# Router, shift vectors and attention combination of a transformer block on one Trainium2 core: three re-orderings and one change of engine

## The chip, the cores and the metric

The kernel runs on one core of a Trainium2 chip. The metric is device microseconds of one execution. The engines are TensorE (PE, with its weight loads shown as PEld), VectorE (DVE), ScalarE (ACT), GpSimd (POOL) and SyncE (SP), which issues most DMAs. All of them run at the same time, each in the order of its own queue, and wait for one another through semaphores.

## The reference

One block of a diffusion transformer, batch 1, 1024 tokens of width 2048 and 256 context tokens. A conditioning vector c is turned by a large matrix `w_ada` (2048 x 12288) into six modulation vectors (shift, scale and gate for two halves); the context has its own c_ctx. Then:

```
mod_x = (silu(c) @ w_ada + b_ada)            # six vectors of 2048; [0] shift, [1] scale
mod_c = (silu(c_ctx) @ w_ada + b_ada)
hx = rmsnorm(x, norm1_g) * (1 + mod_x[1]) + mod_x[0]      # hc the same with mod_c
q, k, v, p, gb, gc, xin = split(hx @ w_in)   # k, v for the context too; q, k turned by rope
# differential attention, 8 heads, two maps each, over 1280 keys
a = softmax(q k / 8);  w = a[map 0] - lam * a[map 1];  att = w @ v
mix = concat(rmsnorm(att), pool_mix(p), gb * conv(gc * xin)) @ w_out
x = x + mod_x[2] * mix
h2 = rmsnorm(x, norm2_g) * (1 + mod_x[4]) + mod_x[3]
aff = softmax(h2 @ w_router)                 # 16 experts
g, idx = top_k(aff.T, 128)                   # each expert takes its 128 best tokens
y = scatter_add(idx, g * (silu(xg @ w_gate) * (xg @ w_up)) @ w_down)
out = rmsnorm(x + mod_x[5] * y, final_g)
```

## The kernel before, in words

Products are made in a split form: an fp32 operand is cut into a high part (ACT copies it to the matmul's type) and a low part (DVE or POOL subtracts), and three products high-high, low-high and high-low stand for one. The weights of the in-projection come in units of 512 KB (`w_unit`, L414: a DMA `w_raw` by SP, an ACT copy L419, a subtraction L420 on an engine that the caller names), two buffers deep.

**In-projection.** Its work is cut into chunks of 128 output columns (`ChunkA`); a chunk has 16 steps, one for each 128 rows of width, and each step has six products `g_x` on 768 token columns (nine with the context columns). The first two chunks run while the inputs and the scale vectors arrive. The scale vectors are made by `ada_block` (L281 to L291): PE multiplies loads of w_ada column by column as they come (`ada_ps`, column-tiled: four products of 32 columns each side by side in one bank), ACT copies the bank to `ada_s`, and four small products `ada_pc` turn it into columns. Next come six plain chunks without the shift (P2, P3, and GB0 to GB3), then K, V, Q, GC and X chunks, in which four extra columns of the token operand hold the shift vectors (`shift_columns`), so that the bias of a chunk comes out of the same products. The shift vectors must therefore be there before the first K chunk. Here they are made by `ada_shift(j)`, j = 0, 1, through `weighted_rows`: 32 loads of 128 x 1024, of which DVE accumulates column 0 (L304) and, for the context, ACT scales (L307) and POOL adds (L308); then 4 x 8 PE transposes (`ada_t`, L314) and DVE sums. `next_rows` starts the next such list. After them come `bias_late`, and the later modulation vectors beside the K to X chunks.

**Attention.** 64 steps (head, block of 256 queries, half of it). A step i does a list of operations taken from `T["even"]`, `T["odd"]`, or for the last 18 steps `T["late"]` and `T["lato"]`: `S` is `score(i + 2)` (PE products `sc` of both maps, DVE maximum `nm` L947, ACT exponential `e` L952), `C` is `combine(i + 2)` (DVE: reciprocal `cf` L959, two small operations, the multiply-add of the two maps L964), `T0` to `T2` transpose step i's combined map (`turn`: `trw`, `wth`, `wtl`), `V` multiplies with v, and a number is a share of filling: pieces of the out-projection and of the pool and conv features that PE does in between. Each `nm` is held behind the last multiply-add by an order edge (`nosync`).

**Router.** Four blocks of 256 tokens: `ln2(b)` normalises (L1279, L1280), transposes and multiplies with the router's weights (`rl`), and `affinity(b)` copies the logits (`lg`), turns them by products with `sel16` (the second `rl`), adds the mean's part (`rsm` L1257), exponentiates, scales (L1265) and turns back (L1266). All of these products share one PSUM buffer, tag `rl`. In front of the first, `rls` is a product of ones with the weights' column sums `sws` (L1236). PE fills the gaps with the out-projection (`fill(n)`: n pieces, a token piece being three or more products `gm`). Top-k runs on DVE in two parts: over the first three blocks (`top(0)`, L1341 to L1350, 768 wide) and over the last and the merge (`top(1)`). Then `chosen` is the list of tokens, which an indirect DMA gathers (L1469).

**Experts.** 16 experts, three matrices each, come as 512 KB or 1 MB loads and are split like the others (ACT L1409, DVE or POOL L1413, `es_t`); the first pieces are prepared before the gather ends. `split` takes four of them on POOL and the rest on DVE.

**Order.** Each engine's order is made by a planner that simulates a time line: of the instructions that are ready, the one that comes first in the program goes first. `nosync` adds an order without a semaphore.

Of the kernel before, what the change touches and what calls it, by code (L numbers as in the profile page):

```python
# [20 lines left out]
P = 128  # L21
# [46 lines left out]
    adm=2,  # L68
# [7 lines left out]
    sh1=0,  # L76
    sh2=0,
# [10 lines left out]
    pin=1,  # L88
    nsy=1,
# [75 lines left out]
def block_kernel(tc, I, out, dbg=None):  # L165
# [127 lines left out]
    def weighted_rows(wap, c0, cols):  # L293

        accs = [p.tile([P, 1024], F32, name="ada_a", tag="ada_a", bufs=1) for _, _, p, _ in cols]
        for k in range(KT):
            wt = wt_pools[ada_n[0] % len(wt_pools)].tile([P, 1024], F32, name="ada_w", tag="ada_w")
            ada_n[0] += 1
            sp.dma_start(wt, wap[k * P:(k + 1) * P, c0:c0 + 1024])
            for (col, eng, _, _), a in zip(cols, accs):  # L300
                if k == 0:
                    act.activation(a, wt, AF.Copy, scale=col(k))
                elif eng is dve:
                    dve.scalar_tensor_tensor(a, wt, col(k), a, op0=ALU.mult, op1=ALU.add)  # L304
                else:
                    t = adx.tile([P, 1024], F32, name="ada_m", tag="ada_m", bufs=T["adm"])
                    act.activation(t, wt, AF.Copy, scale=col(k))  # L307
                    eng.tensor_tensor(a, a, t, op=ALU.add)  # L308
# [13 lines left out]
    def ada_shift(j):  # L322
        ks = slice(8 * j, 8 * j + 8)
        yield from weighted_rows(w_ada, j * 1024, [(lambda k: st[:, k, 0:1], dve, ev, mods[:, 0, ks]),
                                                   (lambda k: st[:, k, 1:2], gp, adx, modc[:, 0, ks])])
        for m in (mods, modc):
            dve.tensor_tensor(m[:, 0, ks], m[:, 0, ks], b_col[:, ks], op=ALU.add)
# [140 lines left out]
    adx = mk("adx", bufs=1, side="left")  # L468
# [93 lines left out]
    rows_left = [ada_shift(0), ada_shift(1), bias_late()] + [ada_late(m, j) for m in (2, 3, 4, 5) for j in range(2)]  # L562
# [12 lines left out]
    next_rows()  # L575
    for n, (g, off, dst) in enumerate([(2, OFF_P, pS), (3, OFF_P, pS)] + [(g, OFF_GB, gbS) for g in range(4)]):
        finish_plain(run_chunk(off + g * P, False, False), dst[g])
        if n == T["sh1"]:
            next_rows()
        if n == T["sh2"]:  # L580
            next_rows(False)
            shift_columns()
            next_rows()
    for h in range(HEADS):
        finish_k(run_chunk(OFF_K + h * P, True), h)
        if h % 2:
            next_rows()
        if h == 0:
            mk.close("adx")
            wt_pools[2:] = [mk("adw", bufs=T["adw"], side="left")] * T["adw"]  # L590
# [87 lines left out]
    pos = {"job": 0, "unit": 0, "tick": 0, "gen": None, "half": 0, "pool": None}  # L678
# [15 lines left out]
    def features(parts, finish, hook):  # L694
# [4 lines left out]
        for u in range(2):  # L699
            s = next_unit()  # L700
            for kk in range(8):
                hi, lo = parts[2 * u + kk // 4]
                for wl, hh in ((0, hi), (0, lo), (1, hi)):
                    one = mm(o, s[:, wl, kk, :], hh[:, kk % 4, :], start=(n == 0), stop=(n == 3 * KT - 1))
                    nosync(tc, one, pos["pin"])
                    n += 1
# [5 lines left out]
    def tokens(b, c, hook):  # L712
# [3 lines left out]
        for j in MIX_ORDER:  # L716
            s = next_unit()
            for kk in range(4):
                n += 1
                hi, lo = mix_parts[b][j]  # L720
                for qt in range(2):
# [4 lines left out]
                    mm(o[:, qt], lo[:, kk, t], s[:, 0, kk, :], start=False, stop=(n == KT))  # L726
# [422 lines left out]
    if True:  # L1149
# [14 lines left out]
        for i in range(LEAD):  # L1164
            score(i)
            fill(T["f3"])
            combine(i)
        want = [0.0]
        waiting = None
        for i in range(NS):  # L1170
# [16 lines left out]
            for op in T[("late" if late else "even") if qt == 0 else ("lato" if late else "odd")]:  # L1187
# [14 lines left out]
                elif op == "C" and nxt:  # L1202
                    combine(nxt)
# [36 lines left out]
    dve.tensor_copy(S2W, t[:, 0:NE])  # L1240
# [6 lines left out]
    def affinity(b, rl):  # L1247
# [16 lines left out]
        for qt in range(2):  # L1264
            dve.tensor_scalar(sm[:, qt], sm[:, qt], sc_[:, 4 + qt:5 + qt], None, op0=ALU.mult)  # L1265
            pe.transpose(r3[0:NE, qt * P:(qt + 1) * P], sm[:, qt], ident)  # L1266
        dve.tensor_copy(affT[:, b * QB:(b + 1) * QB], r3[0:NE, 0:QB])

    def ln2(b):
# [21 lines left out]
        affinity(b, rl)  # L1291
# [112 lines left out]
    def split(i, kk, early=None):  # L1404
        if i < len(units) and (i, kk) not in splits:
# [8 lines left out]
            if early and not on_gp:  # L1414
                nosync(tc, lo, early)
# [32 lines left out]
    for i in range(2):  # L1448
        for kk in range(2):
            split(i, kk, chosen)  # L1450
# [182 lines left out]
```

## Time and profile before

| | us |
|---|---|
| median of three runs | 3376.15 (3362.58 to 3376.82) |
| profiled run | 3386.7 |
| its span, first to last instruction | 3384.9 |
| PE busy | 3084.9 (91%) |
| DVE busy | 2350.6 (69%) |
| ACT busy | 1808.5 (53%) |
| POOL busy | 963.3 (28%) |
| mean granted clock of PE | 0.954 of full speed |

Read by stage (us of the span): input and scale vectors to 93, the first two chunks to 111, six plain chunks to 250, the K to X chunks to about 915, attention to 1896, router to 2155, experts to the end. In the columns of the window view PEclk is the granted clock of PE as a share of full speed, and DMA share is the mean busy share of the 16 DMA engines.

### The profile page before, as it was taken

The page shows a single profiled execution, that of the slowest core. Times are in us where ns is not written, and L with a number is a line of the kernel's source. Part 1 is how long each engine was busy: PE and PEld are TensorE (multiplying, and loading weights), DVE is VectorE, ACT ScalarE, POOL GpSimd, SP SyncE. Part 2 cuts the span into 40 slices and gives each one's busy share as a digit, 9 for nine tenths or more (in the row PEclk, how much of TensorE's full clock was granted, in tenths as well). Part 3 has the DMA queues.
Part 4 walks back from the last instruction along what each step waited for, and adds up shares of the span by engine and source line. Part 5 has one row for each costly group of instructions (what it writes and reads, how often), then busy time and mean ns, then how long its engine had stood idle before and what let it go on. Part 6 is the DMA issues. An engine that isn't in the chain of part 4 may idle for free. (4 is left out here: it accounts for less than half of the span.)

```text
span 3384.9 us, 48355 instructions
## 1 busy us (share of the span) xinstructions
PE 3084.9 (91%) x18527; PEld 2650.1 (78%) x18527; DVE 2350.6 (69%) x2778; ACT 1808.5 (53%) x2585; POOL 963.3 (28%) x608
## 2 busy tenths in 40 slices
PE   7789999999978889888989989599999999999996
PEld 5678989888867778777989879478877777777774
DVE  5666765662157666666555479789888888878877
ACT  5433422362245555554445344577766677667665
POOL 1551100010245544544666576320000000000021
PEclk9899999999989899988999999799999999999998
DMA  9668777732465554646777876899999999999998
GB/s 322 189 184 274 266 261 253 255 124 91 118 188 171 156 160 141 183 130 219 226 258 249 284 261 199 336 342 376 382 374 367 369 358 370 358 370 369 352 328 317
DMA packets 489562, 891.22 MB, mean 263 GB/s; under 512 B 24913, under 2 KB 339874, under 8 KB 478450
## 3 DMA queue, kind: packets, MB, share of 16 engines
q1 hardware_dynamic: 465488, 791.42, 66.9%
q0 software_dynamic: 23744, 96.68, 9.3%
q8 instruction: 145, 2.38, 0.3%
q14 instruction: 87, 0.71, 0.1%
q10 hardware_dynamic: 98, 0.03, 0.0%
HBM read 797.80 MB, written 90.23 MB: 262 GB/s over the span
## 5 line engine op out<-in xcount | busy, mean ns | idle before, releaser
L1413 DVE TENSOR_TENSOR es_t<-er_t,es_t 128x1024 fp32r<-128x1024 f32 x764 | 892.3, 1221 | 103.5 <-ACT es_t L1409 101.9
L1409 ACT CAST es_t<-er_t 128x1024 fp32r<-128x1024 f32 x768 | 776.7, 1052 | 187.0 <-PE gu L172 104.6
L420 POOL TENSOR_TENSOR w_split<-w_raw,w_split 128x1024 fp32r<-128x1024 f32 x208 | 543.2, 2618 | 464.0 <-ACT w_split L419 452.0
L172 PE MATMUL g_x<-hxh,w_split 128*128 128x512 f32 (+3 forms) x2560 | 596.9, 344 | 17.4 <-DVE w_split L420 11.6
L419 ACT CAST w_split<-w_raw 128x1024 fp32r<-128x1024 f32 x288 | 301.6, 1049 | 400.8 <-PE g_x L172 113.7
L172 PEld LDWEIGHTS g_x<-hxh,w_split 128*128 128x128 f32 x2560 | 402.8, 192 | 64.4 <-DVE w_split L420 13.3
L172 PE MATMUL gm<-w_split,mxh 128*128 128x256 f32 x2048 | 391.5, 291 | 11.1 <-DVE oy L1112 5.5
L172 PEld LDWEIGHTS gm<-w_split,mxh 128*128 128x128 f32 x2048 | 327.8, 196 | 17.5 <-issue 6.7
L172 PE MATMUL g_x<-hxl,w_split 128*128 128x256 f32 (+1 forms) x1280 | 338.0, 342 | 1.3 <-DVE hxl L392 1.3
L172 PE MATMUL gu<-es_t,xh 128*128 128x512 f32 x1024 | 293.8, 407 | 22.5 <-DVE es_t L1413 22.5
L172 PE MATMUL dn<-es_t,hh 128*128 128x512 f32 x1024 | 300.4, 405 | 9.7 <-DVE es_t L1413 5.8
L172 PE MATMUL gm<-hbh,w_split 128*128 128x256 f32 x1280 | 277.5, 303 | 21.9 <-ACT e_raw L493 18.9
L172 PE MATMUL gm<-w_split,mxl 128*128 128x256 f32 x1024 | 295.8, 289 | 1.1 <-DMA mxl<-mixP 1.1
L172 PE MATMUL gg<-es_t,xh 128*128 128x512 f32 x1024 | 290.8, 400 | 1.1 <-ACT xh L1479 1.1
L947 DVE TENSOR_REDUCE nm<-sc 128x1 f32<-128x1280 f32 x128 | 190.5, 1488 | 145.7 <-ACT e L952 80.6
L952 ACT ACTIVATE e<-sc,nm 128x1280 f32<-128x1280 f32 x128 | 170.3, 1331 | 182.6 <-DVE nm L947 182.1
L1469 POOL DMA_INDIRECT xg<-h2S,idxT x16 | 22.3, 1391 | 825.0 <-PE tre L1477 675.6
L172 PEld LDWEIGHTS gu<-es_t,xh 128*128 128x128 f32 x1024 | 197.4, 194 | 74.9 <-DVE es_t L1413 27.8
L304 DVE SCALAR_TENSOR_TENSOR ada_a<-ada_w,st,ada_a 128x1024 f32<-128x1024 f32 x150 | 227.3, 1515 | 40.0 <-DMA ada_w<-in_w_ada 36.5
L172 PEld LDWEIGHTS gm<-hbh,w_split 128*128 128x128 f32 x1280 | 219.5, 202 | 33.7 <-ACT e_raw L493 22.0
L172 PEld LDWEIGHTS dn<-es_t,hh 128*128 128x128 f32 x1024 | 190.3, 191 | 61.9 <-DVE es_t L1413 14.9
L172 PEld LDWEIGHTS gg<-es_t,xh 128*128 128x128 f32 x1024 | 190.8, 189 | 47.3 <-DVE es_t L1413 2.1
(303 smaller groups left out, 5323.5 us busy)
## 6 DMA issues: line engine op xcount, KB each, us to landing
er_t<-in_w_gate SPq DMA_DIRECT2D x128, 1024.0 KB, 8.6
er_t<-in_w_down SPq DMA_DIRECT2D x128, 1024.0 KB, 9.2
er_t<-in_w_up SPq DMA_DIRECT2D x125, 1024.0 KB, 12.6
ada_w<-in_w_ada SPq DMA_DIRECT2D x192, 512.0 KB, 5.6
w_raw<-in_w_in SPq DMA_DIRECT2D x160, 512.0 KB, 4.5
w_raw<-in_w_out SPq DMA_DIRECT2D x128, 512.0 KB, 5.3
ks<-kS POOLq DMA_DIRECT2D x16, 1280.0 KB, 8.1
vh<-vS POOLq DMA_DIRECT2D x16, 640.0 KB, 5.5
```

Source lines behind the costliest of these rows:

```text
L172: return pe.matmul(o, l, r, start=start, stop=stop, skip_group_check=True)
L304: dve.scalar_tensor_tensor(a, wt, col(k), a, op0=ALU.mult, op1=ALU.add)
L419: act.copy(s[:, 0], r)
L420: lo_eng.tensor_tensor(s[:, 1], r, raw(s[:, 0]), op=ALU.subtract)
L947: r = dve.tensor_reduce(nm, s, axis=AX, op=ALU.max, negate=True)
L952: act.activation(e, s, AF.Exp, bias=nm, scale=1.0, accum_out=ssum)
L1409: c = act.copy(s[:, 0], r)
L1413: lo = (gp if on_gp else dve).tensor_tensor(s[:, 1], r, raw(s[:, 0]), op=ALU.subtract)
L1469: ins = gp.indirect_dma_start(out=xg, out_offset=None, in_=h2S, in_offset=bass.IndirectOffsetOnAxis(ap=idxT[:, e:e + 1], axis=0))
```

## The change

Four edits. The shift vectors are made on PE by column-tiled products, like the scale vectors, one load of w_ada for each step of the chunks P2 and P3; the accumulation on DVE, ACT and POOL is gone, and with it the pool `adx`. The list of bias rows starts after the first GB chunk, and `shift_columns` after P3. In the attention, `C` stands at the head of the list and combines step i + 1. In the router, `rls` comes after the first block's norm, and PE's two groups of products of each affinity but the last are put behind 5 and 18 pieces of filling, by an order edge to the last piece's product. And the DVE splits of the first six pieces of the experts are held behind `chosen`.

```
-    even=['S', 0.3, 'V', 0.35, 0.0, 'T0', 0.3, 'T1', 'T2', 0.05, 'C'],
-    odd=['S', 0.25, 'T0', 0.4, 'T1', 0.2, 'T2', 'C', 0.15],
-    late=['S', 0.0, 0.0, 'V', 'T0', 0.35, 'T1', 'T2', 0.4, 'C', 0.25],
-    lato=['S', 0.25, 0.0, 'T0', 0.25, 'T1', 'C', 0.5, 'T2'],
+    even=['C', 'S', 0.3, 'V', 0.35, 0.0, 'T0', 0.3, 'T1', 'T2', 0.05],
+    odd=['C', 'S', 0.25, 'T0', 0.4, 'T1', 0.2, 'T2', 0.15],
+    late=['C', 'S', 0.0, 0.0, 'V', 'T0', 0.35, 'T1', 'T2', 0.4, 0.25],
+    lato=['C', 'S', 0.25, 0.0, 'T0', 0.25, 'T1', 0.5, 'T2'],
...
+    gaps=(5, 18),
...
+    def ada_shift():
+        n = 0
+        for j in range(4):
+            pm = pada.tile([P, 512], F32, name="ada_ps", tag="ada")
+            for hb in range(2):
+                c0 = j * 512 + hb * 256
+                for u in range(4):
+                    wt = (adap if n % 4 < 2 else adn).tile([P, 4, 256], F32, name="ada_w", tag="ada_w", bufs=2)
+                    n += 1
+                    sp.dma_start(wt, w_ada[u * 512:(u + 1) * 512, c0:c0 + 256].rearrange("(k p) n -> p k n", p=P))
+                    for g in range(4):
+                        mm(pm[32 * g:32 * g + 32, hb * 256:hb * 256 + 256], st[:, 4 * u + g, :], wt[:, g, :],
+                           start=(u == 0), stop=(u == 3))
+                    if hb == 1 and u == 3:
+                        sb = adn.tile([P, 512], F32, name="ada_s", tag="ada_s", bufs=1)
+                        act.copy(sb, pm)
+                    yield
+                    if hb == 0 and u == 1 and j > 0:
+                        finish(j - 1, last)
+            last = sb
+            def finish(j, sb):
+                pc = tr_bank("ada_pc")
+                for q in range(4):
+                    mm(pc[:, 2 * q:2 * q + 2], sb[:, q * P:(q + 1) * P], sel2)
...
+        finish(3, last)
...
-    def run_chunk(*args):
+    def run_chunk(*args, beside=None):
         c = ChunkA(*args)
         for k in range(KT):
+            if beside:
+                next(beside, None)
             c.step(k)
...
-        finish_plain(run_chunk(off + g * P, False, False), dst[g])
-        if n == T["sh1"]:
-            next_rows()
-        if n == T["sh2"]:
-            next_rows(False)
+        finish_plain(run_chunk(off + g * P, False, False, beside=shifts if n < 2 else None), dst[g])
+        if n == 1:
+            for _ in shifts:
+                pass
             shift_columns()
+        if n == 2:
             next_rows()
...
-            combine(i)
+        combine(0)
...
-                elif op == "C" and nxt:
-                    combine(nxt)
+                elif op == "C" and i + 1 < NS:
+                    combine(i + 1)
...
-    t = pl.tile([P, 512], F32, name="rls", tag="rl", bufs=1)
-    mm(t[:, 0:NE], ones, sws)
+    def shift_logits():
+        t = pl.tile([P, 512], F32, name="rls", tag="rl", bufs=1)
+        nosync(tc, mm(t[:, 0:NE], ones, sws), pos["last"])
+        dve.tensor_copy(S2W, t[:, 0:NE])
...
+        fill(gaps[0])
         for qt in range(2):
-            mm(r2[:, qt], lg[:, qt * P:(qt + 1) * P], sel16)
+            nosync(tc, mm(r2[:, qt], lg[:, qt * P:(qt + 1) * P], sel16), pos["last"] if gaps[0] else None)
...
+        fill(gaps[1])
+        for qt in range(2):
+            nosync(tc, pe.transpose(r3[0:NE, qt * P:(qt + 1) * P], sm[:, qt], ident), pos["last"] if gaps[1] else None)
...
-        affinity(b, rl)
+        if b == 0:
+            shift_logits()
+        affinity(b, rl, T["gaps"])
...
-            if early and not on_gp:
-                nosync(tc, lo, early)
+            if not on_gp and i < 6:
+                nosync(tc, lo, chosen)
```

## Rows read from the trace of the kernel before

**Rows 1.** Page, busy time of TensorE, share of the span, instructions.
```profile
PE 3084.9 (91%) x18527; PEld 2650.1 (78%) x18527; DVE 2350.6 (69%) x2778; ACT 1808.5 (53%) x2585; POOL 963.3 (28%) x608
```

**Rows 2.** Stages: us, busy of PE, PEld, DVE, ACT, POOL, PEclk, DMA share, GB/s.
```profile
114.50:250.10 135.60, 115.57 (x605) 99.22 (x606) 102.18 (x54) 52.07 (x57) 85.64 (x29) 0.89 0.66 194
250.10:915.00 664.90, 656.75 (x4042) 586.57 (x4041) 366.85 (x500) 222.66 (x382) 55.73 (x57) 1.00 0.61 203
915.00:1610.00 695.00, 593.01 (x4291) 528.90 (x4290) 456.26 (x635) 380.80 (x766) 349.08 (x257) 0.91 0.57 171
1896.00:2155.00 259.00, 201.56 (x1702) 188.03 (x1702) 197.82 (x333) 98.54 (x152) 167.37 (x77) 0.89 0.77 263
2155.00:3385.00 1230.00, 1158.14 (x5052) 923.45 (x5050) 1020.74 (x926) 854.59 (x901) 100.63 (x71) 0.97 0.96 359
```

**Rows 3.** PE's timeline, 110 to 165: start, us, operation, [idle before <-releaser].
```profile
114.52 0.62 PE L172 MATMUL g_x<-hxh,w_split 128*128 128x512 f32 x2 [3.54 <-ACT w_split L419]
...
119.71 1.65 PE L172 MATMUL g_x<-hxh,w_split 128*128 128x512 f32 x4 [4.21 <-DVE w_split L420]
...
164.55 1.09 PE L314 MATMUL ada_t<-cst,ada_a 128*128 128x128 f32 x4 [5.49 <-DVE ada_a L304]
```

**Rows 4.** Lines L308 and L420 (100 to 260): duration min/median/max ns, starts.
```profile
L308 POOL TENSOR_TENSOR ada_a<-ada_a,ada_m x30: 2362/3222/3394, 98.0 to 236.3; 128x1024 f32<-128x1024 f32 x30
...
L420 DVE TENSOR_TENSOR w_split<-w_raw,w_split x14: 1212/1558/3409, 116.3 to 254.6; 128x1024 fp32r<-128x1024 f32 x14
```

**Rows 5.** Windows inside the first 201 us.
```profile
0.00:85.00 85.00, 62.81 (x494) 42.64 (x495) 46.83 (x109) 50.83 (x94) 8.98 (x20) 0.96 1.02 322
...
156.00:170.00 14.00, 7.26 (x28) 5.88 (x27) 10.34 (x6) 5.53 (x7) 9.79 (x3) 0.63 0.77 227
170.00:201.00 31.00, 31.00 (x183) 27.21 (x182) 18.46 (x13) 12.02 (x13) 15.21 (x6) 1.00 0.55 160
```

**Rows 6.** Timeline of PE and ACT, 79 to 99, beside the scale vectors.
```profile
79.29 0.95 PE L172 MATMUL ada_pc<-cst,ada_s 128*128 128x2 f32 x8
80.60 2.36 PE L172 MATMUL ada_ps<-ada_w,st 128*32 128x256 f32 x40 [0.37 <-PE ada_pc L172]
...
87.18 0.39 PE L172 MATMUL g_x<-hxh,w_split 128*128 128x512 f32 x1
87.50 0.64 PE L172 MATMUL ada_ps<-ada_w,st 128*32 128x256 f32 x8
88.07 0.62 PE L172 MATMUL g_x<-hxl,w_split 128*128 128x512 f32 x2
...
93.86 1.15 ACT L302 ACTIVATE ada_a<-ada_w,st 128x1024 f32<-128x1024 f32 x1 [8.18 <-DMA ada_w<-in_w_ada]
...
98.81 1.65 PE L172 MATMUL g_x<-hxh,w_split 128*128 128x512 f32 x4 [2.22 <-ACT hxh L391]
```

**Rows 7.** Waits, 925 to 1896: us, times, longest; L964's durations as in rows 4.
```profile
PE sc L172 <- ACT e L952: 20.5, 19, 4.1
...
DVE cf L959 <- ACT e L952: 64.7, 56, 3.1
...
L964 DVE SCALAR_TENSOR_TENSOR e<-e,cf,e x64: 1536/1551/5541, 957.7 to 1861.3; 128x1280 f32<-128x1280 f32 x64
```

**Rows 8.** PE's timeline, router.
```profile
1919.10 0.61 PE L172 MATMUL rls<-sws,ones 128*128 128x16 f32 x2 [3.84 <-DVE sws L1236]
...
2007.00 0.59 PE L1266 MATMUL rl<-cst,rsm 128*16 128x128 f32 x2 [8.13 <-DVE rsm L1265]
```

**Rows 9.** DVE's timeline, router.
```profile
1986.42 10.18 DVE L1279 SCALAR_TENSOR_TENSOR h<-x1r,rst,G 128x2048 f32<-128x2048 f32 x1 [4.65 <-POOL rst L349]
...
2053.24 0.94 DVE L1341 MAX8 vals<-affT 16x8 f32<-16x768 f32 x1
```

**Rows 10.** DVE and PE, end of the top-k and the gather.
```profile
2128.39 2.11 DVE L1413 TENSOR_TENSOR es_t<-er_t,es_t 128x1024 fp32r<-128x1024 f32 x1
2131.22 2.58 DVE L1413 TENSOR_TENSOR es_t<-er_t,es_t 128x1024 fp32r<-128x1024 f32 x1
...
2153.84 1.94 PE L1477 MATMUL tre<-cst,xg 128*128 128x128 f32 x8 [7.76 <-DMA xg<-h2S,idxT]
```

More of the change, by code (lines that the diff above doesn't have):

```diff
@@ L67 @@
     ada2=3,
-    adm=2,
     adw=3,
@@ L75 @@
     plx=2,
-    sh1=0,
-    sh2=0,
     xa=4,
@@ L302, in weighted_rows @@
                     act.activation(a, wt, AF.Copy, scale=col(k))
-                elif eng is dve:
+                else:
                     dve.scalar_tensor_tensor(a, wt, col(k), a, op0=ALU.mult, op1=ALU.add)
[L305 to L308, printed above, removed]
         yield
@@ L320, in ada_late @@
         dve.tensor_tensor(mods[:, m, ks], mods[:, m, ks], b_col[:, m * KT + 8 * j:m * KT + 8 * j + 8], op=ALU.add)
[L322 to L327, printed above, removed]
+    def ada_shift():
[22 more added lines that the diff above has]
+                    mm(pc[:, 2 * q:2 * q + 2], sb[:, q * P:(q + 1) * P], sel2)
+                v = pc[:, 0:8].rearrange("p (q s) -> p s q", s=2)
+                ks = slice(4 * j, 4 * j + 4)
+                for i, m in enumerate((mods, modc)):
+                    dve.tensor_tensor(m[:, 0, ks], v[:, i, :], b_col[:, ks], op=ALU.add)
+        finish(3, last)
     def bias_late():
@@ L467, in block_kernel @@
     ev = mk("ev", bufs=1, side="left")
-    adx = mk("adx", bufs=1, side="left")
+    adn = mk("adn", bufs=2, side="left")
     cosA = ev.tile([P, NA], F32, name="cosA")
@@ L560, in run_chunk @@
         return c
-    rows_left = [ada_shift(0), ada_shift(1), bias_late()] + [ada_late(m, j) for m in (2, 3, 4, 5) for j in range(2)]
+    rows_left = [bias_late()] + [ada_late(m, j) for m in (2, 3, 4, 5) for j in range(2)]
     rows_now = []
@@ L574, in block_kernel @@
         finish_plain(first[g], pS[g])
-    next_rows()
+    shifts = ada_shift()
     for n, (g, off, dst) in enumerate([(2, OFF_P, pS), (3, OFF_P, pS)] + [(g, OFF_GB, gbS) for g in range(4)]):
-        finish_plain(run_chunk(off + g * P, False, False), dst[g])
-        if n == T["sh1"]:
-            next_rows()
-        if n == T["sh2"]:
-            next_rows(False)
+        finish_plain(run_chunk(off + g * P, False, False, beside=shifts if n < 2 else None), dst[g])
+        if n == 1:
+            for _ in shifts:
+                pass
             shift_columns()
+        if n == 2:
             next_rows()
@@ L588, in block_kernel @@
         if h == 0:
-            mk.close("adx")
+            mk.close("adn")
             wt_pools[2:] = [mk("adw", bufs=T["adw"], side="left")] * T["adw"]
@@ L677, in block_kernel @@
     jobs, unit_list, unit_tiles = [], [], {}
-    pos = {"job": 0, "unit": 0, "tick": 0, "gen": None, "half": 0, "pool": None}
+    pos = {"job": 0, "unit": 0, "tick": 0, "gen": None, "half": 0, "pool": None, "last": None}
     due = []
@@ L705, in features @@
                     nosync(tc, one, pos["pin"])
+                    pos["last"] = one
                     n += 1
@@ L725, in tokens @@
                     mm(o[:, qt], hi[:, kk, t], s[:, 1, kk, :], start=False, stop=False)
-                    mm(o[:, qt], lo[:, kk, t], s[:, 0, kk, :], start=False, stop=(n == KT))
+                    pos["last"] = mm(o[:, qt], lo[:, kk, t], s[:, 0, kk, :], start=False, stop=(n == KT))
                     if qt == 1 and kk == 3 and hook:
@@ L1236, in block_kernel @@
     dve.tensor_reduce(sws, sw_.rearrange("p k e -> p e k"), axis=AX, op=ALU.add)
-    t = pl.tile([P, 512], F32, name="rls", tag="rl", bufs=1)
-    mm(t[:, 0:NE], ones, sws)
     S2W = ln.tile([P, NE], F32, name="S2W")
-    dve.tensor_copy(S2W, t[:, 0:NE])
+    def shift_logits():
+        t = pl.tile([P, 512], F32, name="rls", tag="rl", bufs=1)
+        nosync(tc, mm(t[:, 0:NE], ones, sws), pos["last"])
+        dve.tensor_copy(S2W, t[:, 0:NE])
     def router_mm(rl, k, xT):
@@ L1245, in block_kernel, with affinity @@
     last_exp = [None]
-    def affinity(b, rl):
+    def affinity(b, rl, gaps=(0, 0)):
         lg = ln.tile([P, QB], F32, name="lg", tag="lg", bufs=1)
@@ L1265, in affinity @@
             dve.tensor_scalar(sm[:, qt], sm[:, qt], sc_[:, 4 + qt:5 + qt], None, op0=ALU.mult)
-            pe.transpose(r3[0:NE, qt * P:(qt + 1) * P], sm[:, qt], ident)
+        fill(gaps[1])
+        for qt in range(2):
+            nosync(tc, pe.transpose(r3[0:NE, qt * P:(qt + 1) * P], sm[:, qt], ident), pos["last"] if gaps[1] else None)
         dve.tensor_copy(affT[:, b * QB:(b + 1) * QB], r3[0:NE, 0:QB])
@@ L1449, in block_kernel @@
         for kk in range(2):
-            split(i, kk, chosen)
+            split(i, kk, True)
     if "aff" in dbg:
```

## The prediction

> **What bounds the kernel now.** I read the page's busy list first, then the busy windows by stage, then TensorE's (PE's) own timeline in the stretches that the diff touches, and last who waits for whom there. PE is busy 91% of the span [rows 1]. By stage [rows 2] it has 656.75 of 664.90 us in the in-projection's K, V, Q, GC and X chunks and 1158.14 of 1230.00 us in the experts, so both stages are PE's, and whatever is saved ahead of them moves the end one for one. The slack lies in three windows that the diff touches: the six plain chunks with the shift vectors beside them (114.5 to 250.1: 20.0 us idle, and granted clock 0.89), attention (915 to 1610: 102.0 us idle, 0.91), and the router (1896 to 2155: 57.4 us idle, 0.89). The sum is made against the profiled run, 3386.7 us with a span of 3384.9; the median of the runs is 3376.15, 10.6 lower, and I carry the difference over to it.
>
> **Shift vectors.** Before, 32 loads of 512 KB are reduced by 30 multiply-adds on DVE and 30 additions on POOL (2.4 to 3.4 us each [rows 4]), then turned by 32 transposes. The price on PE is not the transposes but the splits of the weights: DVE's w_split takes 1.2 us at its shortest and 3.4 at its longest [rows 4], and PE stands 3.54 and 4.21 us before split weights and 5.49 before a finished accumulator [rows 3]. After such a stop the next products run at half clock for a while: 156 to 170 has 7.26 us busy of 14 at clock 0.63, 170 to 201 has 31.00 of 31 at 1.00 [rows 5]. That last row prices the work: 183 products in 31.00 us, 0.169 us each; six chunks of 96 products are 97.6 us, where the stage took 135.6.
>
> Added on PE: 32 loads with 4 column-tiled products each (8 records). Lying alone between g_x products they move the next one: g_x at 87.18, the eight records at 87.50, g_x at 88.07 [rows 6] is 0.89 us from one to the next, less 0.17 for the first product itself, so 0.7 a load. Forty records in a row take 2.36 us [rows 6], 0.47 a load. The diff hands out one load's products per chunk step, so I take 0.7: 32 x 0.7 = 22.4 us. The Trainium skill, "TensorEngine Tiling (Array Packing)", section Key Properties, says that a change of tiling mode drains TensorE, and it speaks against this edit; the trace agrees as far as 0.7 against 0.47 goes, which is 7 us over the 32 loads, and without the drain the stage would end 7 us sooner. Four finishes of 8 small records each take 0.95 us plus a wait of 0.37 behind the copy of the sums [rows 6]: 4 x 1.3 = 5.3 us. So PE's work is 97.6 + 22.4 + 5.3 = 125 us.
>
> Start: the third chunk's first product came at 114.52 after 3.54 us of waiting for ACT [rows 3]. ACT had stood 8.18 us at an ada_a for a DMA, ahead of a copy for which PE waited, and PE stood 2.22 us more for the modulated input behind it [rows 6]. Neither step is there afterwards, so I start at 110. Unstalled the stage ends at 235 instead of 250.
>
> Now the DMA. The 32 loads (16.8 MB) move out of a stretch of 136 us at 194 GB/s [rows 2] into two chunks, with some 3 MB of weights and rope tables: 20 MB. PE needs 32.5 + 22.4 + 2.6 = 57 us for those two chunks; at 322 GB/s, what loads of this shape reached in the first 85 us [rows 5], 20 MB take 62. That is 5 us of stall, and only 2 + 2 buffers (two of which come free only when the input tiles are released) cost perhaps 1 more: end at 241, gain 9. Bounds: with the products in bunches at 0.47 and no stall the gain is 22. If a load keeps its buffer for 10 us, about what the experts' larger loads need, four buffers bring 200 GB/s: 100 us for the 20 MB, 43 of stall, of which prefetch ahead of the stage and the chunks behind absorb some; I put the far end at a loss of 14. Behind a load that waits for its buffer on SP stand the raw weights of the next chunk, for whose splits DVE and then PE wait; with two weight buffers of eight steps each that is hidden as long as the wait is under a few steps. I take -9, as the nearest row is one of the same shape of load. The steps moved along (bias rows one chunk later, shift columns one chunk later) have DVE and POOL beside them that the accumulations have left, and four chunks without shift ahead of the first use; cost 0. Without that cover the K chunk would stand for the 2 us of POOL copies.
>
> **Combination one step later.** In the program it moves from the end of a step's list to the head of the next step's, past the last filling, the loads of the next q and k and the pool/conv work of a block's end; the next maximum stays behind it by an order edge in both versions. DVE idles 64.7 us ahead of its first instruction, all of it for ACT's exponential, but PE's waits that name the chain are 20.5 us [rows 7]. The order within an engine is made by a planner that issues what is ready first, so a combination that is not ready had already been passed by whatever stood behind it, and no arithmetic is added. The bounds: -25 if the idle time is filled and the scores come free earlier, +38 in the rival below. I take 0, since the position moves past so little.
>
> **Router.** The sum product rls made PE stand 3.84 us for DVE [rows 8], and the half clock after it costs about 2 (by the same 0.63-against-1.00 pattern as in rows 5). Moved behind the first block's filled layer norm, it finds sws ready: -5 to -6. The spread of the next two affinity groups sets filling of 5 units (1.8 us, a unit being three products) and 18 (6.5 us) ahead of the two groups of products. The 8.13 us stop [rows 8] had more filling than this between the two groups and came of a multiply-add that took 10.18 us on DVE [rows 9]; a floor on the filling does not remove it for certain: half of 8.13, and 2 for the clock, is 5, against which stands that a later third affinity makes the first top-k start later than 2053.24 [rows 9], which ends together with PE's filling: +2 to +8. Bounds for the router -16 and +8; I take -6.
>
> **Split order.** Two es_t subtractions of 2.11 and 2.58 us lie inside the last top-k chain on DVE, during which PE has nothing; behind `chosen` they fall into PE's and DVE's wait of 7.76 us for the gather [rows 10]. That is 4.7 us of chain; they need buffers anyway first used after the gather. I take -4, bounds -5 and 0.
>
> Sum: -9 + 0 - 6 - 4 = -19 on 3386.7, 3368; from the median, 3357.
>
> **Rivals.** (A) *Attention's wait is really freed.* For it: 64.7 us of DVE idle time in 56 places; against it: PE idles on many releasers, of which this is one. With 20.5 of PE's waits and about 5 of clock gone: 3357 - 25 = 3332. (B) *The combination at the head of a step delays the next scores.* The multiply-add is 1.55 us [rows 7] and the next maximum lies behind it; if the planner leaves it at the head, waiting, then DVE copies for PE that stood ahead of it come later, and the scores' bank is released later. Half a microsecond to 0.6 in each of 64 steps is 38 us: 3395. It decides from 0.3 us a step on, which eats the 19. For it: PE is busy 85% of that window, so it does wait there; against it: the planner. (C) *The planner had done it already and the loads bind.* Attention, affinity and the filling come out in the order of before, and the shift stage is held by its loads, ending at 248: only rls, the split and 2 us remain, 3376 - 12 = 3364, within measurement of before. That the change then hardly does what it says is in this case.
>
> **How the numbers follow.** The forecast has 0.45, A 0.17, B 0.15, C 0.23. What a measurement of this kernel can tell from no change is 0.5%, 16.9 us: faster is below 3359, slower above 3393. The forecast's own range is 3345 to 3368, two thirds of it below 3359, so faster is 0.30 + 0.17 + 0.02 from C = 0.49; slower is two thirds of B and a share of the shift loss, 0.13; the rest 0.38. The range goes from a little below A to just below B's value: 3325 to 3390.
>
> **What would show it.** Right: no w_split on DVE above 2 us between 110 and 250, the clock at 1.00 there, GB3 ending near 241, PE's waits of 1 us or so for ada_w alone; rls without a gap; pure top-k rounds in the last chain. Wrong: PE waits for ada_w of tens of us; maxima on DVE that come later against the scores, with sc waiting more for e than 20.5 us in total (B) or far less, with the window of attention shorter by over 15 us (A).

## The result and the profile after

The changed kernel takes 3350.14 us (median of 6, 3348.22 to 3354.88), the kernel before 3373.86 us in the same comparison: ratio 0.9929, 95% interval 0.9914 to 0.9945, which is 24 us less (19 to 29). The forecast was 19 less. The profiled run took 3349.46 us, 0.7 under its median, while the profiled run of before lay 12.8 over its own. So the spans differ by 37.2 us (3347.7 against 3384.9), and some 13 of these have nothing to do with the change; they have to be found and taken out before a stretch of the two traces is compared.

The stages of the kernel before, each now from the end of one kind of work to the end of the next. The columns are those of [rows 2]: start and end, us, busy of PE, PEld, DVE, ACT and POOL, granted clock, DMA share, GB/s.

```profile
110.10:246.40 136.30, 112.75 (x590) 96.48 (x589) 103.06 (x53) 54.85 (x60) 87.22 (x29) 0.89 0.65 190
246.40:910.30 663.90, 656.80 (x4036) 586.37 (x4035) 367.28 (x498) 220.50 (x379) 51.39 (x51) 1.00 0.61 204
910.30:1895.50 985.20, 871.98 (x6548) 797.03 (x6547) 603.82 (x841) 519.61 (x987) 545.36 (x359) 0.93 0.63 192
1895.50:2153.80 258.30, 200.91 (x1701) 187.35 (x1699) 198.24 (x334) 98.50 (x151) 167.37 (x77) 0.89 0.77 262
2153.80:3384.90 1231.10, 1159.30 (x5056) 924.64 (x5056) 1020.74 (x926) 854.62 (x901) 100.63 (x71) 0.97 0.96 359
```

The same five stages of the changed kernel:

```profile
108.40:229.70 121.30, 121.29 (x817) 94.80 (x816) 35.60 (x38) 22.26 (x34) 4.02 (x16) 1.00 0.87 273
229.70:890.00 660.30, 655.59 (x4032) 585.98 (x4031) 347.67 (x480) 220.31 (x378) 48.60 (x35) 1.00 0.57 190
890.00:1862.30 972.30, 855.52 (x6548) 783.25 (x6547) 603.71 (x841) 517.57 (x987) 549.87 (x359) 0.95 0.63 194
1862.30:2118.80 256.50, 201.23 (x1701) 187.42 (x1699) 196.01 (x334) 98.00 (x151) 164.12 (x77) 0.90 0.77 265
2118.80:3347.70 1228.90, 1159.05 (x5056) 924.76 (x5056) 1022.08 (x926) 856.63 (x901) 93.80 (x71) 0.97 0.96 360
```

Read the first row of each. PE has 227 more records in the six plain chunks and still needs 15.0 us less for them, because it now is busy in all but 0.01 us, at clock 1.00 instead of 0.89; POOL has fallen from 87 to 4 us and DVE from 103 to 36. No weight split on DVE is late any more (duration ns min/median/max, first and last start; those of before are in [rows 4]):

```profile
L439 DVE TENSOR_TENSOR w_split<-w_raw,w_split x14: 1217/1225/1227, 110.7 to 235.1; 128x1024 fp32r<-128x1024 f32 x14
```

With the start at 108.4 instead of 110.1 the chunks end 16.7 us sooner. That lead then grows by 3.6 us in the K to X chunks, by 12.9 in attention, by 1.8 in the router and 2.2 in the experts. The 12.9 look like the second great effect. They are not: see the runs with one edit each.

In attention, what DVE waits for (engine and line, releaser, us, times, longest) is nearly what it was in [rows 7]: 63.0 for the exponential instead of 64.7, and PE's waits for it 23.7 instead of 20.5.

```profile
PE sc L170 <- ACT e L974: 23.7, 21, 6.7
...
DVE cf L981 <- ACT e L974: 63.0, 57, 2.1
```

In the router the product of the column sums no longer waits, but PE stands twice for the first affinity, and 6.82 us for the second (start, us, operation, idle time before it and its releaser; answering to [rows 8]); the multiply-add of [rows 9] takes 10.17 us, as before. In the first block the same operation takes 2.35 us with nothing on POOL beside it; here POOL issues two DMAs and then runs three splits on end, to 1961.69, and the multiply-add ends 2.16 us behind them:

```profile
1889.60 2.35 DVE L1306 SCALAR_TENSOR_TENSOR h<-x1r,rst,G 128x2048 f32<-128x2048 f32 x1 [0.66 <-DMA acc<-x]
...
1905.33 0.29 PE L170 MATMUL rls<-sws,ones 128*128 128x16 f32 x2
...
1923.64 0.28 PE L1293 MATMUL rl<-cst,rsm 128*16 128x128 f32 x1 [1.39 <-DVE rsm L1290]
...
1925.93 0.28 PE L1293 MATMUL rl<-cst,rsm 128*16 128x128 f32 x1 [2.02 <-DVE rsm L1290]
...
1953.68 10.17 DVE L1306 SCALAR_TENSOR_TENSOR h<-x1r,rst,G 128x2048 f32<-128x2048 f32 x1 [1.68 <-POOL rst L368]
...
1954.70 6.99 POOL L439 TENSOR_TENSOR w_split<-w_raw,w_split 128x1024 fp32r<-128x1024 f32 x3
...
1974.12 0.60 PE L1293 MATMUL rl<-cst,rsm 128*16 128x128 f32 x2 [6.82 <-DVE rsm L1290]
```

At the end of the top-k the two subtractions of [rows 10] have left the chain and stand behind the indices; but PE's wait for the gather has grown from 7.76 to 10.18 us:

```profile
2109.26 0.17 DVE L1476 TENSOR_TENSOR idxT<-lst,trk 128x16 int32<-128x16 f32 x1
2109.35 2.35 DVE L1442 TENSOR_TENSOR es_t<-er_t,es_t 128x1024 fp32r<-128x1024 f32 x2
...
2112.54 1.07 POOL L1498 DMA_INDIRECT xg<-h2S,idxT  x1 [6.85 <-issue]
...
2118.82 1.54 PE L1506 MATMUL tre<-cst,xg 128*128 128x128 f32 x6 [10.18 <-DMA xg<-h2S,idxT]
```

### The profile page after: what moved, and what is told of

The parts are those of the page before. It is cut to its first block, busy times and chain, and to the rows that moved or that the text cites. A ratio compares the mean times of both kernels' runs of the same rounds, so it can differ in the third digit from the quotient of the medians.

```text
span 3347.7 us, 48675 instructions
## 1 busy us (share of the span) xinstructions
PE 3077.1 (92%) x18783; PEld 2634.0 (79%) x18783; DVE 2259.7 (68%) x2744; ACT 1771.7 (53%) x2555; POOL 869.4 (26%) x578
## 5 line engine op out<-in xcount | busy, mean ns | idle before, releaser
L170 PE MATMUL g_x<-hxl,w_split 128*128 128x256 f32 (+1 forms) x1280 | 331.3, 339 | 0.6 <-DVE hxl L411 0.6
L170 PEld LDWEIGHTS gm<-hbh,w_split 128*128 128x128 f32 x1280 | 214.8, 197 | 28.2 <-ACT e_raw L512 16.7
L170 PEld LDWEIGHTS g_x<-hxl,w_split 128*128 128x128 f32 x1280 | 198.0, 189 | 24.1 <-issue 2.5
## 6 DMA issues: line engine op xcount, KB each, us to landing
er_t<-in_w_up SPq DMA_DIRECT2D x125, 1024.0 KB, 12.8
```

What stands on the lines that cost most here:

```text
L170: return pe.matmul(o, l, r, start=start, stop=stop, skip_group_check=True)
```

## The experiments

Theory 1: each edit is worth what its own stretch shows. Theory 2, for the shift vectors and attention: the planner lays attention out anew once the first stage is changed.

### Each edit alone

**Shift vectors alone.** The core of the edit is the new `ada_shift` and its call beside P2 and P3.

```
-    def ada_shift(j):
+    def ada_shift():
...
+        finish_plain(run_chunk(off + g * P, False, False, beside=shifts if n < 2 else None), dst[g])
```

> Only the shift vectors by column-tiled products; combination, router and split order as before. Theory 1 (each edit is worth what its own stretch of the two traces shows): the first K chunk starts some 16 us sooner in the profile, attention keeps its length, and the median is 13 to 18 us below before. Theory 2 (the attention's gain of the whole change, about 10 us between first and last score, comes of the planner laying attention out anew once the shift stage is gone): attention is also about 10 us shorter here, and the median is 20 to 28 us below before.

Measured: 3352.83 us against 3376.9, ratio 0.9933 (0.9913 to 0.9953), 23 us less (16 to 29). That alone is as much as the whole change. In its trace the six chunks take 121.0 us, PE busy throughout:

```profile
109.50:230.50 121.00, 120.99 (x814) 94.35 (x813) 35.59 (x38) 22.28 (x34) 3.96 (x16) 1.00 0.87 272
```

**Combination alone.**

```
-    even=['S', 0.3, 'V', 0.35, 0.0, 'T0', 0.3, 'T1', 'T2', 0.05, 'C'],
+    even=['C', 'S', 0.3, 'V', 0.35, 0.0, 'T0', 0.3, 'T1', 'T2', 0.05],
...
-                elif op == "C" and nxt:
-                    combine(nxt)
+                elif op == "C" and i + 1 < NS:
+                    combine(i + 1)
```

> Only the combination at the head of the next step's list. Theory 1: first to last score about 10 us shorter than before, median 6 to 11 us below before. Theory 2, and the prediction: attention within 3 us of before, median within 4 us. Rival B of the prediction: about 38 us slower.

Measured: 3376.57 us against 3376.9, ratio 1.0001 (0.9987 to 1.0015). More than the time says the order of the instructions. In the two traces the records of PE (18527), DVE (2778), ACT (2585) and POOL (608) and SP's DMA issues (1286) name the same operations and tiles in the same order throughout. The planner had made the move already. DVE's wait for the exponential is 65.2 us:

```profile
DVE cf L959 <- ACT e L952: 65.2, 56, 2.3
```

**Router alone.**

```
+    gaps=(5, 18),
...
+        if b == 0:
+            shift_logits()
+        affinity(b, rl, T["gaps"])
```

> Only the router's edit: the product for the column sums moved behind the first norm, and filling ahead of the affinity products. Theory 1: the stop of 3.84 us before the column sums' product goes, but stops before the affinity products of about the same total take its place, time from the last value product to the end of filling within 2 us of before, median within 3 us. Prediction: that stretch 6 us shorter, median 6 us below before.

Measured: 3372.86 us against 3376.9, ratio 0.9992 (0.9980 to 1.0003): 3 us less at the middle, from 7 less to 1 more. From the last value product to the end of filling 214.3 us, against 216.7 in the profile before and 212.5 and 212.3 in the two runs beside it whose router is that of before (combination alone and split alone). The idle time of PE in that stretch was 20.5 us before, and is 18.3 in this run and 18.3 and 18.4 in those two. The stop for the column sums is gone, and other stops make up for it (waits of PE, us in total, times, longest). The stop for the second affinity is smaller in this kernel, 2.80 us: PE does 186 filling products between its two groups, where the kernel before has 119. But DVE's long wait for POOL has moved to another instruction, a subtraction of 10.03 us, behind which PE stands 3.02 us for `oy`, and the first affinity costs 4.7:

```profile
PE rl L1273 <- DVE rsm L1270: 8.5, 4, 2.8
PE gm L173 <- DVE oy L1114: 3.0, 1, 3.0
```

**Split order alone.**

```
-            if early and not on_gp:
-                nosync(tc, lo, early)
+            if not on_gp and i < 6:
+                nosync(tc, lo, chosen)
```

> Only the DVE subtractions of the experts' first pieces behind the choice. Both theories: the last top-k chain 4 to 5 us shorter, median 3 to 5 us below before. If the subtractions are then late for the first expert, PE stands for es_t after the gather and the gain is 0 to 2 us.

Measured: 3374.69 us against 3376.9, ratio 0.9998 (0.9987 to 1.0009). In the trace the chain from its first maximum to its last takes 19.0 us instead of 23.4, a gain of 4.4; the gather is then issued 3.3 us after the start of the last index operation instead of 1.1, and 2.3 us are left:

```profile
2131.75 0.17 DVE L1447 TENSOR_TENSOR idxT<-lst,trk 128x16 int32<-128x16 f32 x1
2131.83 2.35 DVE L1413 TENSOR_TENSOR es_t<-er_t,es_t 128x1024 fp32r<-128x1024 f32 x2
...
2135.02 1.07 POOL L1469 DMA_INDIRECT xg<-h2S,idxT  x1 [6.79 <-issue]
```

These runs also settle attention. From the first score product to the last the whole change takes 890.5 us and the profiled run of before 901.1. But the router-only and split-only kernels, with attention's code of before, take 893.8 and 892.9, and combination alone, whose order of instructions is that of before, 890.5; shift vectors alone take 889.9. So the difference between the first two traces lies within what one order of instructions shows from run to run. What differs is the granted clock. Before and combination alone, from first to last score, in the columns of [rows 2]:

```profile
948.33:1849.42 901.09, 800.14 (x6005) 726.83 (x6004) 574.87 (x799) 482.85 (x930) 481.30 (x321) 0.93 0.61 186
948.98:1839.50 890.52, 788.68 (x6005) 717.14 (x6004) 572.81 (x800) 482.38 (x930) 481.49 (x322) 0.95 0.61 188
```

PE is idle for 101 and 102 us; the same 6005 records are 11.5 us longer at 0.93 of the clock than at 0.95. Why the clock was lower in that run stays open. The shift edit does change the order of DVE's instructions in attention. But the eight kept traces with shift vectors on PE take 885.9 to 892.9 us there and the six without 890.5 to 901.1; the ranges overlap, so the 10 us of theory 2 are not shown, and a gain of a few us is not ruled out.

### Why the six chunks got faster

**Without the context's sums.** The kernel before, with ACT's scaled copies and POOL's additions left out; the context takes the tokens' shift vector.

```
-                                                   (lambda k: st[:, k, 1:2], gp, adx, modc[:, 0, ks])])
+                                                   ])
```

> The kernel before without the context's shift vector (ACT's scaled copies and POOL's additions of the 32 loads are left out; the context takes the tokens' shift, so that part of the output is not computed). Theory 1 (the plain chunks were slow because DVE's work lies beside POOL's additions and stretches): no weight split on DVE above 1.4 us, no wait of PE for one, and the first K chunk starts 12 to 17 us sooner than the 250 of before although no product is added on PE. Rival (the chunks wait for the loads or for DVE's own queue): splits short, but K starts within 5 us of 250.

Measured: 3339.82 us (one run, 37 below the kernel before beside it; only the stretch is used here). The chunks end at 226.6, 19.8 sooner than before. Splits on DVE and multiply-adds in the kernel before have this spread (duration ns min/median/max, first and last start; the splits are in [rows 4]):

```profile
L304 DVE SCALAR_TENSOR_TENSOR ada_a<-ada_w,st,ada_a x30: 1271/2344/3448, 105.9 to 235.1; 128x1024 f32<-128x1024 f32 x30
```

and without POOL's additions beside them:

```profile
106.90:226.60 119.70, 106.64 (x583) 91.82 (x582) 61.56 (x57) 21.04 (x31) 3.04 (x16) 0.96 0.75 230
...
L420 DVE TENSOR_TENSOR w_split<-w_raw,w_split x15: 1217/1220/1227, 110.3 to 247.4; 128x1024 fp32r<-128x1024 f32 x15
...
L304 DVE SCALAR_TENSOR_TENSOR ada_a<-ada_w,st,ada_a x30: 1279/1285/1287, 102.5 to 202.6; 128x1024 f32<-128x1024 f32 x30
```

The same 30 multiply-adds go from a median of 2344 to 1285 ns, and no split is above 1227. PE still stands 13 us in this stage, 7.2 of them for splits on DVE and 4.9 for finished accumulators; it just stands less. The edit takes away ACT's copies together with POOL's additions, but the trace of before tells them apart: of its 30 multiply-adds the ten with no POOL work beside them took 1271 to 1285 ns, eight of these under ACT's copies, and the 19 that lay beside POOL for more than 0.9 us took 1656 to 3448.

**All sums on DVE.** Both accumulations on DVE, with a complete result.

```
-                                                   (lambda k: st[:, k, 1:2], gp, adx, modc[:, 0, ks])])
+                                                   (lambda k: st[:, k, 1:2], dve, adx, modc[:, 0, ks])])
```

> The kernel before with both accumulations on DVE, POOL and ACT's scaled copies out of them; PE's work as before. Theory 1: multiply-adds at 1.3 us each, 60 of them 77 us, splits at 1.2; DVE holds the stage at about 110 to 120 us of its 136, so K starts at 225 to 240 and the median is 8 to 20 us below before, near to the whole change. Rival (PE's products are what wins): K starts later than 245, median within 5 us of before or above.

Measured: 3358.08 us against 3377.15, ratio 0.9943 (0.9929 to 0.9958), 19 us less. One word, and most of the whole change: DVE does twice as many multiply-adds in 1280 ns each, and the chunks end at 217.7. The lead is partly given back: in the first K chunk PE stands 5.04 us for the shift columns.

```profile
109.20:217.70 108.50, 103.64 (x583) 90.18 (x582) 80.73 (x70) 21.25 (x29) 0.00 (x0) 0.97 0.73 215
217.70:250.00 32.30, 24.92 (x143) 21.63 (x143) 20.36 (x22) 3.28 (x6) 2.56 (x13) 0.92 0.74 231
...
L304 DVE SCALAR_TENSOR_TENSOR ada_a<-ada_w,st,ada_a x59: 1276/1280/1287, 105.5 to 227.2; 128x1024 f32<-128x1024 f32 x59
...
247.69 0.58 PE L172 MATMUL g_x<-hxh,w_split 128*128 128x260 f32 x1 [5.04 <-POOL hxh L409]
```

**Two load buffers.** The whole change with half of the buffers for the 32 loads.

```
-                    wt = (adap if n % 4 < 2 else adn).tile([P, 4, 256], F32, name="ada_w", tag="ada_w", bufs=2)
+                    wt = adap.tile([P, 4, 256], F32, name="ada_w", tag="ada_w", bufs=2)
```

> The whole change with two buffers for the 32 loads instead of 2 + 2. The prediction's stall term was worked out from the bytes and 322 GB/s, and the trace after shows none of it. If buffers are what covers the landing (5.2 us each, two in flight are 202 GB/s at best): the two chunks take 16.8 MB / 202 = 83 us instead of 57, K starts 20 to 26 us later, and PE waits for ada_w. If the loads have slack: K starts within 4 us of the 233.5 after.

Measured: 3342.28 us (one run); the chunks end at 233.3, 3.6 later. By its bound of 4 us the second account holds: the loads have slack. They do come more slowly (217 GB/s from 108 to 170, where the change as it stands has 294), but PE hardly waits for them (0.8 us in all): the planner lets chunk products go ahead, and the last of the column-tiled products run at 212 instead of 168.

```profile
108.70:233.30 124.60, 124.31 (x826) 94.32 (x825) 23.14 (x28) 22.83 (x34) 4.05 (x16) 1.00 0.75 231
...
PE ada_ps L170 <- DMA ada_w<-in_w_ada: 0.8, 1, 0.8
...
L170 PE MATMUL ada_ps<-ada_w,st x260: 376/379/403, 94.8 to 212.4; 128*32 128x256 f32 x130
```

### What the gather waits for

**Gather with memory of its own.** The whole change, with two pools allocated in the other order.

```
+    ex = mk("ex", bufs=1, side="right")
     pm["er1"] = mk("er1", bufs=3, side="right")
-    ex = mk("ex", bufs=1, side="right")
```

> The whole change with the two pools of the experts allocated in the other order, so that the gathered rows do not lie where the third raw piece lies that the two late subtractions read. Theory (half of what the top-k chain wins is given back because the gather waits for these two subtractions on DVE, 2 x 1.2 us): the gather is issued 1.0 to 1.2 us after the indices instead of 3.2, PE's wait ahead of the first transposes falls from 10.2 to about 8 us. Rival (DVE's subtractions hold POOL's descriptor writing, wherever the memory lies): still 3 us.

Measured: 3344.43 us (one run). The gather is issued 0.45 us after the start of the last index operation, with DVE's subtractions running beside it, and PE waits 7.76 us:

```profile
2112.13 0.17 DVE L1476 TENSOR_TENSOR idxT<-lst,trk 128x16 int32<-128x16 f32 x1
2112.21 2.35 DVE L1442 TENSOR_TENSOR es_t<-er_t,es_t 128x1024 fp32r<-128x1024 f32 x2
2112.58 1.81 POOL L1498 DMA_INDIRECT xg<-h2S,idxT  x1 [3.38 <-DVE idxT L1476]
...
2119.27 1.97 PE L1506 MATMUL tre<-cst,xg 128*128 128x128 f32 x8 [7.76 <-DMA xg<-h2S,idxT]
```

So it was the memory: only the order of the pools has changed, and the gather no longer waits for the subtractions. That it is the raw piece they read which lies under the gathered rows follows from the order in which the program allocates; no trace shows addresses. Timed:

> The whole change with the gathered rows in memory of their own, timed. From its trace 2.4 us between the last maximum and the first expert's transposes: median 2 to 3 us below the whole change's 3350, a ratio to before of 0.992, inside the interval of the whole change. Rival (the experts' loads, which wait for memory, start later with the other allocation): 3350 or above.

Measured: 3346.24 us against 3374.74, ratio 0.9928 (0.9909 to 0.9948). From the last maximum to the first transposes it takes 9.9 us instead of 12.2 in the change; a gain of this size is too small for the interval to show.

### The router's stops

**Filling by block.**

```
-        affinity(b, rl, T["gaps"])
+        affinity(b, rl, ((5, 30), (5, 90), (5, 18))[b] if b < 3 else (5, 18))
```

> The whole change with the filling ahead of the transposes set by block: 30, 90 and 18 pieces instead of 18 for each. If too little filling is what left PE standing at the second affinity (6.8 us) and the first (3.4 us): both stops go, last value product to end of filling 6 to 10 us shorter than 217.5, median 5 to 9 us below 3350. Rival (the same stops come back elsewhere, or DVE's first top-k, which is busy throughout, then ends last): that stretch within 3 us, median within 3 us of 3350.

Measured: 3366.0 us against 3379.53, ratio 0.9959 (0.9943 to 0.9975); by the ratios some 10 us are lost against the change. PE stands where it stood (1.40 and 2.02 us for the first affinity, 7.52 for the second), and the third affinity comes later: the first top-k begins 171.0 us after the last value product instead of 158.6, and ends 19 us behind the filling, where it ended with it. So the run does not test its theory. The floors of 30 and 90 put no more filling ahead of the transposes: 80 and 137 products lie between the two groups of the first and the second affinity, as in the change. What grew is the filling ahead of the third affinity, 337 products instead of 230.

```profile
1975.75 0.60 PE L1293 MATMUL rl<-cst,rsm 128*16 128x128 f32 x2 [7.52 <-DVE rsm L1290]
...
2036.20 0.95 DVE L1370 MAX8 vals<-affT 16x8 f32<-16x768 f32 x1
...
2101.44 0.94 DVE L1375 FIND_INDEX8 idxu<-vals,work 16x8 uint32<-16x768 f32 x1
```

**Router as before.** The gather with memory of its own, shift vectors and split order as changed, the router as it was.

> The same with the router as before (product of the column sums ahead of the first norm, no filling set ahead of the affinity products). If the router's edit only moved PE's stops, this is within 3 us of the kernel beside it, and the stops of 1.8 to 3.8 us for the column sums and 7 to 8 us for the second affinity are back while those at the first affinity (3 to 5 us) are gone. The prediction's term: 6 us slower than the kernel beside it.

Measured: 3352.08 us against 3374.74, ratio 0.9939 (0.9917 to 0.9961). The medians differ by 5.8 us from the kernel beside it, but the intervals overlap. In the traces the stretch from the last value product to the end of filling is 217.2 us here and 215.8 there, with stops of 3.85 us for the column sums and 6.53 for the second affinity here, 1.40, 2.01 and 7.25 us for affinities there. What the router's edit is worth stays between nothing and its forecast of 6; the trace speaks for 1 to 2.

### A version shared out between DVE and PE

The first 1024 columns accumulated on DVE, the last 1024 made on PE, the gather with memory of its own.

```
-        for j in range(4):
+        for j in range(2, 4):
...
+    def ada_shift_rows():
+        ks = slice(0, 8)
+        yield from weighted_rows(w_ada, 0, [(lambda k: st[:, k, 0:1], dve, ev, mods[:, 0, ks]),
+                                            (lambda k: st[:, k, 1:2], dve, adn, modc[:, 0, ks])])
```

> The whole change with the shift vectors shared out: the first 1024 columns accumulated on DVE (both vectors, nothing on POOL), the last 1024 by column-tiled products on PE, and the gather's memory apart from the raw pieces. If PE's products are the only price left in the stage (20 us for 32 loads) and DVE's accumulation costs PE nothing without POOL beside it: the K chunks start 7 to 10 us before the 229.7 after, and with 2.4 us from the gather the median is 8 to 13 us below the whole change's 3350. Rival (the loads bind, or the shift columns come too late for K, as with all sums on DVE, where PE stood 5 us for them): K's lead is lost again before the K to X chunks end, median within 4 us of 3350.

Measured: 3348.39 us against 3379.53, ratio 0.9917 (0.9900 to 0.9934): not told apart from the change. PE has 5 us less to do, but it stands again, up to 2.2 us at a time, for a load, a copy and a split, and the chunks end at 232.0.

```profile
109.70:232.00 122.30, 116.01 (x689) 94.65 (x689) 72.01 (x68) 21.78 (x32) 2.03 (x16) 0.96 0.86 276
```

No version is shown to beat the changed kernel.

## Why the prediction was right, and where its terms were off

The forecast, 19 us less, lies at the edge of the measured 19 to 29. The sign holds, and so does the main mechanism: PE no longer stands for DVE in the plain chunks. That the total came so near is partly luck, because a shift term that was too small and router and split terms that were too large made up for each other. Of its four terms:

- **Shift vectors, -9: right in kind, too small.** Alone it gives -23 (-29 to -16) in time, and 16 to 17 us in its own stretch of two traces. Over more traces, the first product on context columns in the first K chunk comes at 249.9 to 253.5 in four with the shift vectors of before, and at 233.5 to 239.6 in six with the edit as it stands: some 15 us sooner by the means. The step that was mis-sized is the stall: "That is 5 us of stall", and 1 more for the buffers. Nothing of it came: PE was idle for 0.01 us in the stage, and for 1.2 us at 97 for such a load. The sum of bytes and rate was not wrong in its rate: 282 GB/s from 108 to 140 and 305 from 140 to 168 are below the 322 taken. But it tied the loads to two chunks. Some 8 loads' products already ran before 112, the first of them in the wait for the last scale vectors, and with two buffers the planner spread the rest out, to 212, rather than let PE stand. The other terms were near: the start 108.4 to 109.5 (110 forecast); the column-tiled products 18.3 and 18.7 us from the start of each group to the next product without the waits for loads, in both traces in 24 groups instead of the 32 assumed (22.4 forecast); 16.8 us for the 96 products of a chunk where none lie between (16.3); about 1 us for each finish (1.3). The prediction only noted that the splits were late; that POOL's work beside DVE made them so is shown by the kernels without POOL's additions.
- **Combination, 0: right, and for its reason.** The order of instructions is the same. Rivals A and B (3332 and 3395) fell together; what looked like A in the trace after was the lower clock in the profiled run of before. Rival C was right about the planner in attention and wrong about the loads, which bound nothing.
- **Router, -6: right for rls, wrong for the affinities.** The product for the column sums lost its stop of 3.84 us. The step that failed is "a floor on the filling does not remove it for certain: half of 8.13". In the whole change it removes none of it: 6.82 us, where the shift edit without the router's has 6.93. In two kernels with the floor, router alone and the shared version, the stop is 2.80 and 3.00, with 186 products between the groups instead of 137, and the stretch is no shorter for it. What the prediction left out is why the multiply-add in front of `rsm` takes 10.17 us: it lies beside POOL's splits, as the splits of the first stage did, and with POOL idle it takes 2.35. In those two kernels a subtraction stands in its place and takes 10.03 and 7.65 us, where it takes 1.21 with POOL idle. No run takes POOL's splits away here, so what that would give is not shown. And the first affinity, which had no stop, got two (3.4 to 4.7 us): 69 to 80 products lie between its groups instead of 102, and a multiply-add ahead of the second `rsm` takes 3.41 us instead of 2.35, beside POOL again. The late column sums are not the cause; they were copied 2.9 us before the first `rsm` began. The danger named beside it, a first top-k that begins later, decides as soon as the third affinity moves: with the floor of 90 it came 12 us later, and the gather's rows 14 us later.
- **Split order, -4: half of it.** "They fall into PE's and DVE's wait of 7.76 us for the gather": they do, but the gather waited for them, through a buffer that shares its memory. The chain gained 4.4 and lost 2.1.

The terms that the traces show add up to 17 + 0 + 1 to 2 + 2 = 20 to 21 us, inside the measured interval. Whether the remaining 3 us are real stays open. Some may lie in the K to X chunks, for which the prediction had no term: from the first product on context columns to the first score, six traces with the shift edit take 692.2 to 695.9 us and four with the shift vectors of before 695.5 to 698.7. The ranges touch, and no run tests it.

## What to carry to other kernels

Where two engines share work in one stage, ask what each costs the other's instructions first: one word that took POOL out of the accumulation gave 19 of the 24 us without a single new product. Ask it again wherever one instruction is much longer than its like: the 10 us multiply-add of the router was taken as given, and it too lay beside POOL. Check that filling set ahead of an instruction comes to lie there: with a floor of 90 pieces PE did the same 137 products as with 18. Look also at the memory that a waiting DMA will write. And before a difference between two traces is given to an edit, look at the same stretch in runs that don't have the edit: here 7 to 11 us of attention belonged to none, and between two runs of one order of instructions the granted clock differed.

## What the runs showed of the hardware

DVE's fp32 multiply-add over 128x1024 took 1271 to 1287 ns with POOL idle and up to 3448 ns beside POOL's additions; its subtractions of the same size 1217 to 1227 ns and up to 3409. Beside two DMA issues and three subtractions of POOL on end (6.99 us), a multiply-add over 128x2048 took 10.17 us instead of 2.35, and in the router-only kernel a subtraction over 128x1024 took 10.03 instead of 1.21. They ended 2.16 and 1.1 us behind the last of POOL's, about what they take by themselves. The reverse is there too. In the kernel before, a multiply-add that began 0.18 us ahead of a POOL subtraction took its 2.35 us, and the subtraction 4.43 instead of 2.4:

```profile
1968.15 2.35 DVE L1279 SCALAR_TENSOR_TENSOR h<-x1r,rst,G 128x2048 f32<-128x2048 f32 x1 [0.65 <-POOL rst L349]
...
1968.33 4.43 POOL L420 TENSOR_TENSOR w_split<-w_raw,w_split 128x1024 fp32r<-128x1024 f32 x1 [0.21 <-ACT w_split L419]
```

That reads as one waiting for the other, not as both running slower. It is a reading of these traces, and no run tests it.

A group of column-tiled products between chunk products, in the trace after:

```profile
119.60 0.51 PE L170 MATMUL g_x<-hxh,w_split 128*128 128x512 f32 x2
120.04 0.64 PE L170 MATMUL ada_ps<-ada_w,st 128*32 128x256 f32 x8
120.61 0.62 PE L170 MATMUL g_x<-hxh,w_split 128*128 128x512 f32 x2
```

From its start to the next chunk product is 0.57 us, and it starts 0.09 later than a chunk product would (0.44 instead of 0.35 for the two ahead of it): 0.66 us, where a group in a row takes 0.47 [rows 6]. The Trainium skill, "TensorEngine Tiling (Array Packing)", Key Properties, names a drain at each change of tiling mode, and the trace agrees, at about 0.2 us a group.

And profiled runs of one order of instructions in attention differed by 11 us in 901, at granted clocks of 0.93 and 0.95.
